# Seven products per 2x2 blocks in twelve of the 22 value-gate pairs of block 2's MLP

## The chip, the core and the metric

The kernel runs on one core of a Trainium2 chip. The metric is the device time of one execution in microseconds. Durations come from one profiled execution, which has a time of its own beside the timed runs.

## What is computed

The reference runs two transformer blocks over 512 tokens of width 1024 in float32. The change concerns the MLP at the end of block 2, a gated MLP of width 2816 with a causal convolution of three taps on the value half:

```
u = rmsnorm_2(x, norm_ffn_w)
up, gate = split(u @ w_ffn_up)          # 1024 -> 2 x 2816
a = causal_dwconv_2(up, ffn_conv_w, ffn_conv_b)
x = x + (silu(a) * gate) @ w_ffn_down   # 2816 -> 1024
return rmsnorm_2(x, norm_final_w)
```

The MLP of block 1 is `x + square(relu(rmsnorm(x) @ w1)) @ w2` with width 4096.

## The kernel before

Everything lies transposed, features on the 128 partitions and the 512 tokens along the row, so x is eight tiles of 128x512. Each float32 product is three matmuls (`mm3`, L461 to L463): both operands are split into a rounded high part (type fp32r) and the low rest, and hi by hi, lo of one by hi of the other and the reverse are summed in PSUM.

**Weights.** `weight_order` lists all 128x128 weight tiles in the order of use; eight tiles are a unit of 512 KB. SP loads units into four `raw` buffers, in program order; ScalarE (ACT) casts each to `whi` (L258), VectorE (DVE) subtracts to get `wlo` (L260). There are five buffers for `whi` and five for `wlo`, and one is free again when TensorE (PE) has done its last matmul with it. `defer(n, f)` puts a step off by n weight tiles.

**Plain pairs.** `hidden2(i)` computes value tile i and gate tile 22+i: two units, `lin` over eight k each, so 2 x 8 x 3 = 48 matmuls of 512 columns into two of the four `mm` banks of PSUM. Then DVE multiplies by the norm's factor `rb` (L1676, into `zp`), ACT and DVE do the three taps (L1585, L1587 twice), ACT the silu (L1678), DVE the product with the gate out of PSUM (L1679), and ACT and DVE split the result (L529, L530). `GROUPS2` cuts the 22 pairs into groups of 8, 8 and 6. After each of the first two groups, with the first pair of the next group ahead of it, eight tiles of the down projection follow (L1691 on DVE, L1692 on POOL); the last group ends in a tail by halves of the tokens.

**Pairs by seven products.** The MLP of block 1 already computes 14 of its 16 pairs of output tiles with `pairg`. It takes a pair's weights and the input as 2x2 blocks (two output tiles by two k tiles; two k tiles by two halves of 256 tokens), and needs seven block products instead of eight: 7 x 4 x 3 = 84 matmuls of 256 columns. The list SEVEN gives the order of the products: 1, 5, 2, 7, 3, 6, 4. The weight side (`seven_steps`, L297 to L318) is two sums and their splits: tiles called `a` (products 1 and 4), `s75s` (5 and 7), `s64s` (6 and 3), each of 1024 columns, and `b` (product 2), of 512. The token side (`rights`, L405 to L416) is made once per MLP, in four steps of two x tiles each. A pair fills four banks of PSUM; ACT copies product 1 out (`c0`, L380), and DVE assembles the results in `q` (L386 to L389).

**What sets the order.** SP keeps the program's order. On the other engines a scheduler places the instructions by its own estimates of when their inputs are there, so a step can stand ahead of work that the code writes first. Each engine then takes its instructions strictly in that order.

Of the kernel before, what the change touches and what calls it, by code (L numbers as in the profile page):

```python
# [9 lines left out]
F32 = mybir.dt.float32  # L10
F32R = mybir.dt.float32r
I32 = mybir.dt.int32
U8 = mybir.dt.uint8
AF = mybir.ActivationFunctionType
ALU = mybir.AluOpType
# [3 lines left out]
T = 512  # L19
# [33 lines left out]
VD = 4  # L53
# [6 lines left out]
def weight_order():  # L60
# [12 lines left out]
    def cols(name, ns, ks):  # L73
        for n in ns:
            for k in ks:
                seq.append((name, k, n))
# [6 lines left out]
    r8 = range(8)  # L83
# [32 lines left out]
    cols("w_mix_out_2", r8, r8)  # L116
    for g, (a, b) in enumerate(GROUPS2):
        for i in range(a + (1 if g else 0), b + (1 if b < 22 else 0)):
            cols("w_ffn_up_2", [i, 22 + i], r8)
        cols("w_ffn_down_2", r8, range(a, b))  # L120
    return seq, seven

# [13 lines left out]
            yield 1, 4 * g + 7, g + 1  # L136


GROUPS2 = [(0, 8), (8, 16), (16, 22)]


# [27 lines left out]
def _build(ctx, tc, nc, A, out, stage):  # L169
# [5 lines left out]
    V, S, G, PE = nc.vector, nc.scalar, nc.gpsimd, nc.tensor  # L175
    cnt = [0]

    def nm(s):
        cnt[0] += 1
        return f"{s}_{cnt[0]}"  # L180

    def t2(dt=F32, shape=(P, T)):
        return ap_.tile(list(shape), dt, tag="t2", bufs=NSLOT, name=nm("t2"))
# [10 lines left out]
    def tinyc(n):  # L194
        return ap_.tile([P, n], F32, tag=nm("tinyc"), bufs=1, name=nm("tinyc"))

    def bank(kind="mm"):
        return pp.tile([P, T], F32, tag=kind, bufs=4, name=nm(kind))
# [21 lines left out]
    def col(name, i=0, n=1):  # L220
        o = COFF[name][0] + i
        return colt[:, o:o + n]
# [210 lines left out]
    def defer(n, fn):  # L433

        late.append((wst["i"] + n, fn))
        late.sort(key=lambda e: e[0])
# [37 lines left out]
    def lin(name, n, ks, mv, ps=None, start=True, stop=True, off=0):  # L474
        if ps is None:
            ps = bank()
        for _ in ling(name, n, ks, mv, ps, start, stop, off):
            pass
        return ps
# [56 lines left out]
    def zpad():  # L536
        zp = ap_.tile([P, T + 4], F32, tag="t2", bufs=NSLOT, name=nm("zp"))
        G.memset(zp[:, 0:4], 0.0)
        return zp
# [92 lines left out]
    def acc_tile():  # L632
        return ap_.tile([P, T], F32, tag="t2", bufs=NSLOT, name=nm("acc"))


    xs = []
# [16 lines left out]
    rb = row_bc(rc, 4)  # L653
# [22 lines left out]
    kf, qf, vf, gv, gu, gate, ys = [], [], [], [], [], [], []  # L676
# [540 lines left out]
    xs = xs2  # L1217
# [86 lines left out]
    xs = xs2  # L1304
# [4 lines left out]
    rops, steps = rights(x, "norm_ffn", xs)  # L1309
# [92 lines left out]
    xs = xs2  # L1402

    rc12, rc, rb, rb1 = tinyc(8), tinyc(4), acc_tile(), acc_tile()
# [178 lines left out]
    def conv3(zp, wname, j):  # L1583
        c = tmp()
        S.activation(c, zp[:, 2:2 + T], AF.Copy, scale=col(wname, 3 * j))  # L1585
        for i in (1, 2):
            V.scalar_tensor_tensor(out=c, in0=zp[:, 2 + i:2 + i + T], scalar=col(wname, 3 * j + i),  # L1587
                                   in1=c, op0=ALU.mult, op1=ALU.add)
        return c
# [76 lines left out]
    xs = xs2  # L1666


    rb = acc_tile()
    wide_later(acc, 1e-5, rb, 3, False)  # L1670

    def hidden2(i):
        ps = lin("w_ffn_up_2", i, range(8), xs)
        psg = lin("w_ffn_up_2", 22 + i, range(8), xs)
        zp = zpad()
        V.tensor_mul(zp[:, 4:], ps, rb)  # L1676
        c = conv3(zp, "ffn_conv_w_2", i)
        S.activation(c, c, AF.Silu, bias=col("ffn_conv_b_2", i))  # L1678
        V.tensor_mul(c, c, psg)  # L1679
        return split(c)  # L1680

    hs = []
    for g, (a, b) in enumerate(GROUPS2):
        hs += [hidden2(i) for i in range(a + (1 if g else 0), b)]
# [10 lines left out]

    a, b = GROUPS2[2]
    nk = b - a
# [25 lines left out]
    for hf in range(2):  # L1723
# [4 lines left out]
        st = {}  # L1728
# [140 lines left out]
```

## Time and profile before

| | us |
|---|---|
| runs, median of 3 (lowest to highest) | 1544.16 (1543.84 to 1545.23) |
| the profiled execution: time | 1543.86 |
| the profiled execution: span, first to last instruction | 1542.1 |
| TensorE busy in the span | 1514.8 |
| VectorE busy | 999.0 |
| ScalarE busy | 674.9 |

The span of the profiled execution is 1.8 us under its own time, and that time is 0.3 us under the median of the runs. Busy times of the engines overlap. A matmul's recorded length contains its drain, so what a matmul costs is read from one start to the next; the same holds in part for DVE and ACT, where the next instruction often starts some 0.1 us before the last one is over.

### The profile page before, as it was taken

The numbers are of one execution on the slowest core, as the hardware profiler recorded it, in microseconds if no ns is written. First come the engines' busy times: TensorE is split into PE (matmuls) and PEld (weight loads), VectorE is DVE, ScalarE is ACT, GpSimd is POOL, SyncE is SP. The second block draws the span as 40 slices with busy tenths as digits, with TensorE's granted clock in tenths as the row PEclk, the third lists the DMA queues.
The fourth block names the chain that finished last, engine by engine and source line by source line (L and its number), as shares of the span: only waits on it lengthen the run. The fifth ranks groups of instructions, "written<-read, shape, count | busy, mean of one in ns | idle before, by whom it ended". The sixth has DMA issues, their size and how long they took to land.

```text
span 1542.1 us, 20324 instructions
## 1 busy us (share of the span) xinstructions
PE 1514.8 (98%) x7904; PEld 1274.9 (83%) x7904; DVE 999.0 (65%) x1623; ACT 674.9 (44%) x1117; POOL 143.5 (9%) x162
## 2 busy tenths in 40 slices
PE   8999999999999999999999999999999999999996
PEld 6888898888888888989888888888888888888886
DVE  6897675554786786767688767335546555555557
ACT  6666555443564353535444444333334331332233
POOL 0002120200201212011400000000020002001101
PEclk9999999999999999999999999999999999999998
DMA  6033335221223323324043222222232222232311
GB/s 254 20 111 100 112 130 197 96 68 55 82 72 106 96 95 109 104 83 137 14 150 131 83 82 83 81 92 92 92 96 96 96 96 96 96 96 92 100 41 56
DMA packets 51505, 149.89 MB, mean 97 GB/s; under 512 B 9552, under 2 KB 14032, under 8 KB 51408
## 3 DMA queue, kind: packets, MB, share of 16 engines
q1 hardware_dynamic: 51264, 148.32, 29.1%
q8 instruction: 62, 1.02, 0.3%
q14 instruction: 35, 0.29, 0.1%
q10 hardware_dynamic: 144, 0.26, 0.1%
HBM read 143.97 MB, written 3.28 MB: 95 GB/s over the span
## 4 chain that ended last, share of the span: by engine, by line
PE 95%; DVE 2%; ACT 2%; issue 1%; DMA 0%; POOL 0%; SPq 0%; DVEq 0%; ACTq 0%; POOLq 0%
PE mm L461 28%; PE mm L462 27%; PE mm L463 27%; PE sm L463 2%; PE sm L461 2%; PE sm L462 2%; ACT whi L258 0%; ACT t L1090 0%; DVE wlo L260 0%; DMA raw<-wts 0%; PE sm L581 0%; PE sm L1576 0%; PE sm L1575 0%; PE sm L1577 0%; PE sm L713 0%
## 5 line engine op out<-in xcount | busy, mean ns | idle before, releaser
L461 PE MATMUL mm<-t,whi 128*128 128x512 f32 (+1 forms) x1888 | 719.9, 381 | 9.1 <-ACT whi L254 7.3
L462 PE MATMUL mm<-t,whi 128*128 128x512 f32 (+1 forms) x1888 | 716.7, 380 | 0.2 <-DVE t L530 0.2
L463 PE MATMUL mm<-t,wlo 128*128 128x512 f32 (+1 forms) x1888 | 716.8, 380 | 0.0
L258 ACT CAST whi<-raw 128x1024 fp32r<-128x1024 f32 x226 | 236.5, 1051 | 432.7 <-PE mm L462 286.2
L461 PEld LDWEIGHTS mm<-t,whi 128*128 128x128 f32 x1888 | 355.3, 188 | 77.9 <-ACT whi L254 7.3
L463 PEld LDWEIGHTS mm<-t,wlo 128*128 128x128 f32 x1888 | 355.3, 188 | 72.1 <-DVE wlo L260 0.8
L462 PEld LDWEIGHTS mm<-t,whi 128*128 128x128 f32 x1888 | 355.2, 188 | 69.6 <-DVE t L530 0.4
L260 DVE TENSOR_TENSOR wlo<-raw,whi 128x1024 fp32r<-128x1024 f32 x219 | 287.4, 1312 | 81.8 <-ACT whi L258 78.8
L575 POOL TENSOR_TENSOR acc<-acc,tmp 128x512 f32<-128x512 f32 (+1 forms) x37 | 52.7, 1432 | 468.2 <-ACT tmp L571 467.9
L1436 DVE TENSOR_TENSOR tmp<-mm,acc 128x512 f32<-128x512 f32 x46 | 31.7, 689 | 48.8 <-PE mm L463 46.8
L1393 POOL TENSOR_TENSOR res<-res,tmp 128x512 f32<-128x512 f32 x24 | 39.0, 1638 | 247.9 <-DVE tmp L1391 217.3
L310 DVE TENSOR_TENSOR wlo<-sraw,whi 128x1024 fp32r<-128x1024 f32 x28 | 38.4, 1375 | 26.5 <-ACT whi L305 26.5
L461 PE MATMUL sm<-t,whi 128*128 128x256 f32 (+1 forms) x176 | 50.4, 286 | 1.8 <-ACT whi L305 1.8
L1676 DVE TENSOR_TENSOR zp<-mm,acc 128x512 f32<-128x512 f32 x22 | 15.2, 691 | 55.0 <-PE mm L463 54.9
L463 PE MATMUL sm<-t,wlo 128*128 128x256 f32 (+1 forms) x176 | 50.4, 286 | 0.0
L462 PE MATMUL sm<-t,whi 128*128 128x256 f32 (+1 forms) x176 | 50.2, 285 | 0.0
L305 ACT CAST whi<-sraw 128x1024 fp32r<-128x1024 f32 x28 | 29.3, 1047 | 45.8 <-PE mm L462 41.0
L1692 POOL TENSOR_TENSOR res<-res,tmp 128x512 f32<-128x512 f32 x16 | 20.7, 1294 | 260.2 <-DVE tmp L1691 260.2
L1679 DVE TENSOR_TENSOR tmp<-tmp,mm 128x512 f32<-128x512 f32 x22 | 15.1, 687 | 43.4 <-PE mm L463 42.6
L1391 DVE TENSOR_TENSOR tmp<-mm,acc 128x512 f32<-128x512 f32 x32 | 21.6, 686 | 26.5 <-PE mm L463 22.6
L1691 DVE TENSOR_TENSOR tmp<-mm,acc 128x512 f32<-128x512 f32 x16 | 11.1, 692 | 39.2 <-PE mm L463 39.2
L461 PEld LDWEIGHTS sm<-t,whi 128*128 128x128 f32 x176 | 33.1, 188 | 2.5 <-ACT whi L305 2.0
(379 smaller groups left out, 1840.2 us busy)
## 6 DMA issues: line engine op xcount, KB each, us to landing
raw<-wts SPq DMA_DIRECT2D x259, 512.0 KB, 3.7
res<-xT SPq DMA_DIRECT2D x16, 256.0 KB, 5.2
yT<-t SPq DMA_DIRECT2D x6, 256.0 KB, 2.3
tmp<-tmp SPq DMA_DIRECT2D x20, 64.0 KB, 2.0
gm<-gm SPq DMA_DIRECT2D x4, 256.0 KB, 5.2
dn<-ch SPq DMA_DIRECT2D x4, 256.0 KB, 2.3
tmp<-memT SPq DMA_DIRECT2D x4, 256.0 KB, 2.6
cst<-const SPq DMA_DIRECT2D x1, 576.0 KB, 6.7
```

The lines of the kernel that those rows point to most:

```text
L258: S.copy(hi, r)
L260: defer(LO, lambda r=r, hi=hi, lo=lo: V.tensor_sub(lo, r, hi.bitcast(F32)))
L305: S.copy(t[n][0], s)
L310: V.tensor_sub(t[n][1], src(), t[n][0].bitcast(F32))
L461: PE.matmul(ps, lhsT=ahi, rhs=bhi, start=start, stop=False)
L462: PE.matmul(ps, lhsT=ahi, rhs=blo, start=False, stop=False)
L463: PE.matmul(ps, lhsT=alo, rhs=bhi, start=False, stop=stop)
L575: eng.tensor_add(acc[:, :w], acc[:, :w], dst[:, :w])
L1391: V.tensor_mul(t, ps, rb2)
L1393: G.tensor_add(x[n], x[n], t)
L1436: V.tensor_mul(t, ps, rb)
L1692: G.tensor_add(x[n], x[n], t)
```

## The change

Twelve pairs of block 2 (`SEVEN2`) go through `pairg`; the ten others stay plain. Their weights are listed in `pair` order, `rights` is called for block 2's x with its steps from 5 weight tiles on, and `hidden7` takes the place of `hidden2`: it draws `q` from `pairg` and does the same convolution, silu, product and split from there, with the sign folded into L1695. All twelve use the banks called `sm`; block 1 alternates between `mm` and `sm`.

```
+SEVEN2 = {3, 4, 6, 7, 9, 10, 12, 13, 15, 16, 18, 19}
...
-            cols("w_ffn_up_2", [i, 22 + i], r8)
+            if i in SEVEN2:
+                pair("w_ffn_up_2", i, 22 + i)
+            else:
+                cols("w_ffn_up_2", [i, 22 + i], r8)
...
+    rops2, steps = rights(x, "norm_ffn_w_2", xs)
+    for j, f in enumerate(steps):
+        defer(5 + VD * (j // 3) + j % 3, f)
+
+    def hidden7(i):
+        hl = (t2(F32R), t2(F32R))
+
+        def then(q):
+            zp = zpad()
+            V.tensor_mul(zp[:, 4:], q[:, :T], rb)
+            st = {}
+
+            def taps():
+                st["c"] = conv3(zp, "ffn_conv_w_2", i)
+
+            def gate():
+                c = st["c"]
+                S.activation(c, c, AF.Silu, bias=col("ffn_conv_b_2", i))
+                defer(1, lambda: V.scalar_tensor_tensor(out=c, in0=q[:, T:], scalar=-1.0, in1=c,
+                                                        op0=ALU.mult, op1=ALU.mult))
+                defer(2, lambda: S.copy(hl[0], c))
+                defer(4, lambda: V.tensor_sub(hl[1], c, hl[0].bitcast(F32)))
+
+            defer(1, taps)
+            defer(2, gate)
+
+        for _ in pairg("w_ffn_up_2", i, 22 + i, rops2, then, "sm"):
+            pass
+        return hl
...
     def hidden2(i):
+        if i in SEVEN2:
+            return hidden7(i)
```

A line of before has a number five higher in the changed kernel, and 37 higher behind `hidden7` (L461 is L466, L258 is L263, L305 is L310, L380 is L385, L1678 is L1715).

On PE, where pair 1 of block 2's MLP ends and pair 2 begins, before reads as follows (`mm_10631` is the gate of pair 1, `mm_10662` the value of pair 2, `t` the split x, `whi` and `wlo` the weights):

```order
L461 MATMUL mm_10631<-t_1981_10454,whi_10590 128x512
L462 MATMUL mm_10631<-t_1982_10455,whi_10590 128x512
L463 MATMUL mm_10631<-t_1981_10454,wlo_10591 128x512
L461 MATMUL mm_10662<-t_1933_10183,whi_10634 128x512
L462 MATMUL mm_10662<-t_1934_10184,whi_10634 128x512
L463 MATMUL mm_10662<-t_1933_10183,wlo_10635 128x512
```

In the changed kernel, at the same place, 12 matmuls of pair 3's product 1 (`sm_10807`) and 9 of its product 5 (`sm_10825`, whose `t` are made by `rights`) stand between the gate of pair 1 and the value of pair 2 (`mm_10707`); these are their last six and what follows:

```order
L466 MATMUL sm_10825<-t_2011_10558,whi_10726 128x256
L467 MATMUL sm_10825<-t_2012_10559,whi_10726 128x256
L468 MATMUL sm_10825<-t_2011_10558,wlo_10727 128x256
L466 MATMUL sm_10825<-t_2019_10589,whi_10726 128x256
L467 MATMUL sm_10825<-t_2020_10590,whi_10726 128x256
L468 MATMUL sm_10825<-t_2019_10589,wlo_10727 128x256
L466 MATMUL mm_10707<-t_1933_10183,whi_10666 128x512
L467 MATMUL mm_10707<-t_1934_10184,whi_10666 128x512
```

So 21 matmuls of the first pair by seven products moved ahead of a whole plain pair.

On ACT, behind the silu of pair 0, before reads so (`whi` from `raw` is the cast of a unit of weights, `t` from `tmp` the high part of a pair's result):

```order
L258 CAST whi_10709<-raw_10632 128x1024
L529 CAST t_2001_10552<-tmp_10546 128x512
L1585 ACTIVATE tmp_10621<-zp_10618,colt 128x512
L258 CAST whi_10740<-raw_10663 128x1024
L1678 ACTIVATE tmp_10621<-tmp_10621,colt 128x512
L529 CAST t_2013_10627<-tmp_10621 128x512
L258 CAST whi_10784<-raw_10707 128x1024
```

In the changed kernel the same stretch holds the casts of the pairs by seven products: `whi_10827` and `whi_10858` are `s75s` and `s64s` of pair 4, `t_2060_10755` is `b` of pair 3, and `tmp_10697` belongs to the plain pair 1:

```order
L310 CAST whi_10827<-sraw_10808 128x1024
L1590 ACTIVATE tmp_10697<-zp_10694,colt 128x512
L310 CAST whi_10858<-sraw_10839 128x1024
L1715 ACTIVATE tmp_10697<-tmp_10697,colt 128x512
L534 CAST t_2045_10703<-tmp_10697 128x512
L310 CAST t_2060_10755<-raw_10708 128x512
L1590 ACTIVATE tmp_10789<-zp_10786,colt 128x512
```

The cast of pair 3's `b` moved behind a cast for pair 4 and behind the whole activation of pair 1. The buffer that `whi_10858` takes is that of pair 3's `s75s`.

## Rows read from the trace of the kernel before

**Rows 1.** The page: PE's busy time, and the chain that ended last, by engine.

```profile
PE 1514.8 (98%) x7904; PEld 1274.9 (83%) x7904; DVE 999.0 (65%) x1623; ACT 674.9 (44%) x1117; POOL 143.5 (9%) x162
...
PE 95%; DVE 2%; ACT 2%; issue 1%; DMA 0%; POOL 0%; SPq 0%; DVEq 0%; ACTq 0%; POOLq 0%
```

**Rows 2.** Stretches of block 2's MLP: length, busy us (instructions) by engine, clock, DMA.

```profile
1159.00:1195.00 36.00, 36.00 (x156) 28.82 (x155) 26.24 (x34) 16.17 (x20) 0.00 (x0) 1.00 0.27 88
1195.00:1260.00 65.00, 65.00 (x283) 52.68 (x282) 33.39 (x42) 22.92 (x29) 0.00 (x0) 1.00 0.30 97
```

**Rows 3.** DVE in time order, plain pairs: start, length, line, idle before [releaser].

```profile
1209.87 0.69 DVE L1676 TENSOR_TENSOR zp<-mm,acc 128x512 f32<-128x512 f32 x1 [2.84 <-PE mm L463]
...
1211.90 1.53 DVE L1587 SCALAR_TENSOR_TENSOR tmp<-zp,colt,tmp 128x512 f32<-128x512 f32 x2
1215.49 0.69 DVE L1679 TENSOR_TENSOR tmp<-tmp,mm 128x512 f32<-128x512 f32 x1 [2.06 <-PE mm L463]
...
1226.61 0.69 DVE L1679 TENSOR_TENSOR tmp<-tmp,mm 128x512 f32<-128x512 f32 x1 [2.06 <-PE mm L463]
```

**Rows 4.** PE in time order: first matmuls of two consecutive block-1 pairs.

```profile
447.39 0.28 PE L461 MATMUL sm<-t,whi 128*128 128x256 f32 x1
...
457.31 0.28 PE L461 MATMUL mm<-t,whi 128*128 128x256 f32 x1
```

**Rows 5.** DVE in time order: preparation and assembly of pairs in block 1.

```profile
556.41 0.68 DVE L387 TENSOR_TENSOR q<-mm,q 128x512 f32<-128x512 f32 x1
557.01 1.21 DVE L310 TENSOR_TENSOR wlo<-raw,whi 128x1024 fp32r<-128x1024 f32 x1
558.14 0.41 DVE L388 TENSOR_TENSOR q<-mm,q 128x256 f32<-128x256 f32 x1
558.48 0.68 DVE L315 TENSOR_TENSOR sraw<-sraw,raw 128x512 f32<-128x512 f32 x1
```

**Rows 6.** PE in time order: where it waited among block 1's pairs.

```profile
441.12 0.39 PE L461 MATMUL mm<-t,t 128*128 128x256 f32 x1 [1.54 <-ACT t L305]
...
469.58 0.39 PE L461 MATMUL sm<-t,whi 128*128 128x256 f32 x1 [1.83 <-ACT whi L305]
...
554.56 0.51 PE L461 MATMUL mm<-t,whi 128*128 128x512 f32 x1 [0.64 <-ACT t L380]
...
639.74 0.50 PE L461 MATMUL mm<-t,whi 128*128 128x512 f32 x1 [0.68 <-ACT t L380]
```

**Rows 7.** ACT in time order, just before two of those waits ended.

```profile
439.50 1.04 ACT L305 CAST whi<-sraw 128x1024 fp32r<-128x1024 f32 x1
440.45 0.61 ACT L305 CAST t<-raw 128x512 fp32r<-128x512 f32 x1
...
553.20 1.04 ACT L258 CAST whi<-raw 128x1024 fp32r<-128x1024 f32 x1
554.15 0.36 ACT L380 COPY t<-mm 128x256 f32<-128x256 f32 x1
```

**Rows 8.** DVE in time order at the start of block 2's MLP.

```profile
1159.10 0.69 DVE L1661 TENSOR_TENSOR res<-res,mm 128x512 f32<-128x512 f32 x1 [2.78 <-PE mm L463]
...
1164.45 0.69 DVE L623 TENSOR_SCALAR tmp<-sm 128x512 f32<-128x512 f32 x1 [0.59 <-PE sm L617]
...
1171.78 0.69 DVE L1676 TENSOR_TENSOR zp<-mm,acc 128x512 f32<-128x512 f32 x1
```

**Rows 9.** DVE in time order: first and last instruction of one step of `rights`, block 1.

```profile
415.90 0.42 DVE L411 TENSOR_TENSOR t<-t,t 128x256 f32<-128x256 f32 x1
...
417.82 0.69 DVE L530 TENSOR_TENSOR t<-t,t 128x512 fp32r<-128x512 f32 x1
```

**Rows 10.** The clock: the last stretch (columns of rows 2), and PE's first matmuls.

```profile
1530.00:1542.00 12.00, 0.70 (x2) 0.30 (x2) 6.84 (x15) 0.45 (x2) 1.74 (x2) 0.63 0.26 87
...
9.63 0.63 PE L463 MATMUL mm<-t,wlo 128*128 128x512 f32 x1
10.06 0.63 PE L461 MATMUL mm<-t,whi 128*128 128x512 f32 x1
```

## The prediction

> **What bounds the kernel now.** I read the page first: PE is busy 98% of the span and holds 95% of the chain that ended last [rows 1], so time is won only by giving PE less to do and lost wherever PE is made to wait. Next, the stretches of block 2's MLP [rows 2]: PE is busy without a gap in both, while DVE is busy 26.2 of 36 us in the first (norm, first three pairs) and 33.4 of 65 us in the second (plain pairs). Then the pace of a plain pair: the gate products L1679 of two pairs start 11.12 us apart, and before each DVE stands idle for 2.06 and 2.84 us, waiting for PE [rows 3]. So DVE and ACT are fed by PE here and cost nothing yet. Last, what a pair by seven products costs where the kernel has them: first matmul to first matmul 9.92 us [rows 4], and the places where PE waited for them [rows 6].
>
> **What is removed.** 48 matmuls of 512 columns become 84 of 256: 11.12 - 9.92 = 1.20 us less PE per pair [rows 3, 4], 12 pairs, **-14.4 us**. All of it lies on the path. It is there in full only if PE never waits, so the rest of the sum is waits.
>
> **What is added to DVE and ACT.** From start to start a DVE instruction on 1024 elements takes 1.13 us, one on 512 0.60, one on 256 some 0.35 [rows 5]. Per pair by seven: preparation 4 x 1.13 + 3 x 0.60 = 6.3, assembly 3 x 0.60 + 0.35 = 2.2, then the product with `rb`, two taps (1.5, [rows 3]), the product with the gate and the low part, 3.3; together 11.8 us against PE's 9.92. A plain pair asks 2 x 1.13 + 3.3 = 5.6 against 11.12. A plain pair and two by seven give DVE 29.2 us in PE's 31.0. In the sum it fits, with little slack; what matters is the order in which things stand, and there I see four places.
>
> **Place 1, ahead of pair 2.** 21 matmuls of pair 3 now stand before pair 2 on PE (first change of order shown above). They need `rights`, and pair 2 itself needs the bank that DVE frees with pair 0's `zp`. Counting from the residual of the last mix tile (1159.1, [rows 8]), DVE must do until that `zp`: seven 1024-wide steps of weights 7.9; residual, split, sums and the like, eight 512-wide, 5.0; the root chain, 1164.45 to 1171.78 less the one 1024-wide step inside it, 6.2 [rows 8]; three steps of `rights` at 1.9 for the first five plus two low parts, 3.1 each [rows 9], 9.3; `zp` 0.6. That is 29.0 us. PE comes there after four units (22.2), two sums over partitions (0.5) and 21 matmuls (2.5), at 25.6 with 0.4 lost since the norm's sum comes later. If DVE never waits, PE waits 3.4 us; if DVE waits for ACT's high parts as it does in block 1's opening, up to 6.1. I take **4.9**, the middle, **plus 0.4**. In the queue behind PE's wait is everything of MLP 2.
>
> **Place 2, inside pair 3.** PE finishes pair 2 (T), ends products 5 and 7 at T+1.8 and wants `b`. ACT (second change of order): cast of `s75s` of pair 4, whose buffer pair 2's gate holds until T, done at T+1.2; first tap of pair 1, T+1.9; cast of `s64s` of pair 4, free only after product 7, T+2.9; silu of pair 1, which waits for two taps on DVE that stand behind the low part of `s75s` (1.1 + 1.5), T+4.7; product and low part in between, high part of pair 1, T+6.3; `b`, T+6.9. PE waits 5.1, and 0.4 more for `b`'s low part on DVE. The same order in block 1 (cast of `sraw`, then `b` at once, [rows 7]) cost 1.54 [rows 6]; here an activation chain of a plain pair stands between. If DVE's part were free, ACT alone would leave 2.9. I take **5.5** (2.9 to 5.6), since each link is an instruction in a fixed order.
>
> **Place 3, pairs 15 and 16.** Here too `b` of pair 15 stands behind the cast of `s64s` of pair 16, which waits for pair 15's product 7, and behind one 512-wide cast: 1.0 + 0.5 + 0.6 after product 7, 2.3, plus 0.6 for the low part; and 0.5 at pair 16's start. **3.4** (2.3 to 3.6).
>
> **Place 4, starts of second pairs.** Pairs 4, 7 and 13 follow a pair that used the same four banks. Product 1 needs `c0` copied, product 2 the third assembly step, and on ACT `c0` stands behind a cast that waits for the end of the pair before. The like cost 0.64 and 0.68 in block 1, where the copy stood behind a cast on ACT [rows 6, 7]. By the same walk: pair 4 0.9, pairs 6 and 7 1.2, pairs 12 and 13 0.6; **2.7** (0 to 4). Pairs 9, 10, 18 and 19 have their weights split under the down tiles and cost nothing; if that cover went they would cost what 6 and 7 do, 1.2 each time.
>
> **The clock.** The idle of 1.83 us in block 1 [rows 6] left PE's pace as it was: 11.12 / 48 = 0.23 us from one matmul of 512 columns to the next [rows 3]. At the end of the run PE is all but idle and the mean granted clock is 0.63 [rows 10], so it fell to its lower level; at the start, at that level, such matmuls stand 0.43 apart [rows 10]; the run's first eight do, which is 8 x 0.20 = 1.6 us, and I take that for the price of a fall. Places 1 and 2 have idles of 4 to 5 us, longer than any in the trace before its end. Two falls are 3.2; some 0.8 of it comes back as DVE catches up before pair 4. I take **2.4** (0 to 4.5). The Trainium skill (TensorE: Matmul & The Clock Gate, Part 1: The HAM clock gate) says that half rate is the default state, that activity lifts it and that an idle stretch brings it back, which speaks against a change that trades matmuls for waits. By the trace's longest harmless idle alone the sum would be 2.4 us less, by the page's rule as it stands. The last stretch agrees with the page; whether the idles of places 1 and 2 are of that kind, no run here shows.
>
> **The sum.** DMA: bytes and units are the same, SP's order too; nothing. POOL: only the same clears. So 0.4 + 4.9 + 5.5 + 3.4 + 2.7 + 2.4 = 19.3 of waits against 14.4 gained: +4.9. On the profiled execution's own 1543.9 that gives **1548.8 us**; this execution is 0.3 us under the median, which changes nothing. Low ends together: 8.6 of waits, 1538.1; high ends: 0.4 + 6.1 + 5.6 + 3.6 + 4 + 4.5 = 24.2, 1553.7.
>
> **Rivals.**
> *The waits are there but short*: DVE keeps pace as in the sum of works and the clock holds; 9 to 15 us of waits, 1538 to 1545. For it: DVE's overlap from start to start is often better than I count. Against: place 2 is an order, not a load.
> *Faster, as in block 1*: its 14 pairs cost PE five waits, 1.54 + 1.83 + 0.64 + 0.68 [rows 6] and one of 0.18, 4.9 us in all, 0.35 a pair. Twelve at that rate are 4.2, so 1543.9 - 14.4 + 4.2 = 1533.7. It decides if pair 1's silu and high part are done before product 7, so that `b` follows the `s64s` cast at once and place 2 shrinks to 1.5. Against: the silu's taps wait for a buffer that pair 2 holds.
> *Slower still, DVE is the bound*: by recorded lengths a triple asks DVE 13.0 + 13.0 + 6.0 = 32.0 us against 31.0, and casts beside POOL's work take longer; five triples lose 5 us beyond the high sum's middle, 1554 to 1560.
> *It doesn't do what it says*: the order has 432 more rows on PE, 12 x 36, so it does.
>
> **How the numbers follow.** A difference of 0.2%, 3.1 us, is what a measurement of this kernel can tell from none: faster is under 1541.1, slower over 1547.2. The forecast (1546 to 1553) 0.47, of which 0.06 lies under 1547.2; short waits 0.27, of which 0.07 under 1541.1; block 1's rate 0.12; DVE bound 0.14. Faster 0.12 + 0.07 = 0.19; same 0.20 + 0.06 = 0.26; slower 0.41 + 0.14 = 0.55. The range 1539 to 1555 leaves out block 1's rate and about half of the DVE case, 0.2. Cases of both signs: the forecast's own range is 1546 to 1553.
>
> **What would show it.** In the changed profile: `sm` groups of L466 to L468 with 1008 more matmuls of 256 columns, 576 fewer of 512; PE idle before pair 2 ended by DVE (`t` or `zp`), 4 to 6 us; idle inside pair 3 ended by ACT's 512-wide cast L310, about 5 us; some 2 to 3 us at pair 15 by the same line; a granted clock under 1.00 in the stretch of the first pairs. Wrong would be PE idle under 10 us in MLP 2, or waits that L263 or DMA end.

## The result: 0.5% slower

| | before | changed |
|---|---|---|
| median of 5 runs, us | 1544.16 (1543.44 to 1545.23) | 1551.35 (1550.25 to 1555.27) |
| changed to before | | 1.0053, 95% interval 1.0037 to 1.0070 |
| profiled execution, us | 1543.86 | 1555.27 |
| its span | 1542.1 | 1553.5 |

The forecast was 1548.8 us with a range of 1539 to 1555, and slower as the likeliest sign. The median lies 7.2 us over before, the profiled execution 11.4; it is the slowest of its five, and where its surplus comes from stands at the end of the next section.

### The profile page after: what moved, and what is told of

Same layout as the page of the kernel before. It is cut to its first block, busy times and chain, and to the rows that moved or that the text cites. A ratio compares the mean times of both kernels' runs of the same rounds, so it can differ in the third digit from the quotient of the medians.

```text
span 1553.5 us, 21399 instructions
## 1 busy us (share of the span) xinstructions
PE 1512.2 (97%) x8336; PEld 1292.5 (83%) x8336; DVE 1080.4 (70%) x1759; ACT 705.8 (45%) x1169; POOL 147.9 (10%) x162
## 4 chain that ended last, share of the span: by engine, by line
PE 88%; DVE 6%; ACT 3%; issue 1%; DMA 1%; SPq 0%; POOL 0%; DVEq 0%; ACTq 0%; POOLq 0%
PE mm L466 23%; PE mm L468 23%; PE mm L467 23%; PE sm L468 4%; PE sm L466 4%; PE sm L467 4%; DMA raw<-wts 1%; ACT whi L263 1%; DVE wlo L315 1%; DVE wlo L265 1%; ACT whi L310 1%; ACT t L1095 0%; DVE wlo L267 0%; PE sm L586 0%; DVE t L1807 0%
## 5 line engine op out<-in xcount | busy, mean ns | idle before, releaser
L466 PE MATMUL mm<-t,whi 128*128 128x512 f32 (+1 forms) x1696 | 646.6, 381 | 10.3 <-ACT whi L259 6.7
L468 PE MATMUL mm<-t,wlo 128*128 128x512 f32 (+1 forms) x1696 | 643.2, 380 | 1.9 <-DVE wlo L267 1.4
L467 PE MATMUL mm<-t,whi 128*128 128x512 f32 (+1 forms) x1696 | 642.9, 379 | 0.2 <-DVE t L535 0.2
L466 PEld LDWEIGHTS mm<-t,whi 128*128 128x128 f32 x1696 | 320.2, 189 | 71.2 <-ACT whi L259 6.7
L468 PEld LDWEIGHTS mm<-t,wlo 128*128 128x128 f32 x1696 | 320.2, 189 | 67.3 <-DVE wlo L267 2.7
L467 PEld LDWEIGHTS mm<-t,whi 128*128 128x128 f32 x1696 | 320.3, 189 | 61.5 <-DVE t L538 0.5
L263 ACT CAST whi<-raw 128x1024 fp32r<-128x1024 f32 x202 | 211.3, 1051 | 303.3 <-PE mm L467 138.6
L265 DVE TENSOR_TENSOR wlo<-raw,whi 128x1024 fp32r<-128x1024 f32 x189 | 236.5, 1252 | 78.1 <-ACT whi L263 77.7
L466 PE MATMUL sm<-t,whi 128*128 128x256 f32 (+1 forms) x464 | 132.0, 285 | 4.2 <-ACT t L534 2.3
L467 PE MATMUL sm<-t,whi 128*128 128x256 f32 (+1 forms) x464 | 131.7, 284 | 0.5 <-DVE t L535 0.5
L468 PE MATMUL sm<-t,wlo 128*128 128x256 f32 (+1 forms) x464 | 131.7, 284 | 0.0
L310 ACT CAST whi<-sraw 128x1024 fp32r<-128x1024 f32 x52 | 54.5, 1048 | 88.0 <-PE mm L467 69.3
L466 PEld LDWEIGHTS sm<-t,whi 128*128 128x128 f32 x464 | 88.1, 190 | 5.9 <-ACT t L534 2.5
L467 PEld LDWEIGHTS sm<-t,whi 128*128 128x128 f32 x464 | 88.2, 190 | 1.6 <-DVE t L535 0.7
L468 PEld LDWEIGHTS sm<-t,wlo 128*128 128x128 f32 x464 | 88.2, 190 | 0.4
L310 ACT CAST whi<-raw 128x1024 fp32r<-128x1024 f32 x26 | 27.3, 1050 | 67.7 <-PE mm L467 37.0
L466 PE MATMUL sm<-t,t 128*128 128x256 f32 (+1 forms) x156 | 47.0, 302 | 7.3 <-ACT t L310 7.0
L302 DVE TENSOR_TENSOR sraw<-raw,raw 128x1024 f32<-128x1024 f32 x26 | 33.0, 1269 | 25.3 <-DMA raw<-wts 25.2
```

The costliest lines, as they stand in the source:

```text
L263: S.copy(hi, r)
L265: defer(LO, lambda r=r, hi=hi, lo=lo: V.tensor_sub(lo, r, hi.bitcast(F32)))
L302: V.tensor_tensor(t["s75"].rearrange("p (a b) -> p a b", a=2), r3, r1[:, T:].unsqueeze(1).to_broadcast([P, 2, T]), op=ALU.add)
L310: S.copy(t[n][0], s)
L466: PE.matmul(ps, lhsT=ahi, rhs=bhi, start=start, stop=False)
L467: PE.matmul(ps, lhsT=ahi, rhs=blo, start=False, stop=False)
```

## The profile after

First the page: busy time by engine, and the chain that ended last. They answer to [rows 1].

```profile
PE 1512.2 (97%) x8336; PEld 1292.5 (83%) x8336; DVE 1080.4 (70%) x1759; ACT 705.8 (45%) x1169; POOL 147.9 (10%) x162
...
PE 88%; DVE 6%; ACT 3%; issue 1%; DMA 1%; SPq 0%; POOL 0%; DVEq 0%; ACTq 0%; POOLq 0%
```

PE is 2.6 us less busy, not 14.4, and 7 points of the chain have gone from PE to the others: there are waits now, and something has stretched the matmuls. The stretches of [rows 2] show both (length, busy us and instructions of PE, its weight loads, DVE, ACT, POOL, then the granted clock, DMA):

```profile
1159.00:1195.00 36.00, 31.35 (x138) 25.30 (x137) 29.30 (x48) 17.11 (x23) 1.42 (x6) 0.95 0.17 59
1195.00:1260.00 65.00, 59.73 (x372) 54.23 (x371) 51.53 (x71) 30.05 (x41) 0.41 (x4) 0.92 0.27 90
1191.20:1198.00 6.80, 6.10 (x14) 4.79 (x15) 3.52 (x6) 3.35 (x4) 0.10 (x1) 0.50 0.00 0
```

In before PE was busy for all of both stretches at a clock of 1.00. Now it is idle for 4.65 and 5.27 us of them, the granted clock is 0.95 and 0.92, and for the 6.8 us of the third line it is 0.50, the lower of its two levels (1.2 in place of 2.4 GHz). PE in order of time, the places at which it waited and what followed the second (start, length, idle before and its releaser):

```profile
1188.70 0.39 PE L466 MATMUL sm<-t,whi 128*128 128x256 f32 x1 [2.34 <-ACT t L534]
...
1189.59 0.39 PE L467 MATMUL sm<-t,whi 128*128 128x256 f32 x1 [0.50 <-DVE t L535]
...
1191.90 0.80 PE L466 MATMUL mm<-t,whi 128*128 128x512 f32 x1 [1.81 <-DVE zp L1713]
1192.49 0.63 PE L467 MATMUL mm<-t,whi 128*128 128x512 f32 x1
1192.92 0.63 PE L468 MATMUL mm<-t,wlo 128*128 128x512 f32 x1
...
1212.64 0.58 PE L466 MATMUL sm<-t,t 128*128 128x256 f32 x1 [4.81 <-ACT t L310]
...
1388.44 0.39 PE L466 MATMUL sm<-t,t 128*128 128x256 f32 x1 [2.16 <-ACT t L310]
...
1389.86 0.58 PE L468 MATMUL sm<-t,t 128*128 128x256 f32 x1 [0.33 <-DVE t L315]
```

The first three are place 1, ended by the parts of `rights` (L534, L535) and by pair 0's `zp`; 1212.64 is place 2 and 1388.44 place 3, both ended by the cast of `b` (L310). Behind 1191.90 the matmuls of 512 columns stand 0.43 us apart where they stood 0.23. ACT in order of time ahead of 1212.64 (columns as above) is the queue that the forecast walked through:

```profile
1205.92 1.05 ACT L310 CAST whi<-sraw 128x1024 fp32r<-128x1024 f32 x1 [0.59 <-PE mm L467]
1206.88 0.72 ACT L1590 ACTIVATE tmp<-zp,colt 128x512 f32<-128x512 f32 x1
1207.80 1.04 ACT L310 CAST whi<-sraw 128x1024 fp32r<-128x1024 f32 x1 [0.21 <-PE sm L467]
1209.71 0.72 ACT L1715 ACTIVATE tmp<-tmp,colt 128x512 f32<-128x512 f32 x1 [0.86 <-DVE tmp L1592]
1211.45 0.62 ACT L534 CAST t<-tmp 128x512 fp32r<-128x512 f32 x1 [1.01 <-DVE tmp L1716]
1211.97 0.61 ACT L310 CAST t<-raw 128x512 fp32r<-128x512 f32 x1
```

`b`, the last line, needs nothing but its raw weights, and stands behind two casts for pair 4 and the activation of pair 1 (tap, silu, high part); both casts, the silu and the high part each wait for another engine.

**The account.** All matmuls are in both traces (7904 and 8336), so the MLP, with some 85 us ahead of it, can be measured on PE from the 5801st matmul, the same product in every kernel, to the last: 1074.01 to 1530.43 in before, 1076.52 to 1541.84 after, 456.4 and 465.3 us, +8.9. The gain is there: away from waits and falls a matmul of 512 columns takes 0.232 us and one of 256 takes 0.118 in both traces (medians from start to start), so twelve pairs save 12 x (48 x 0.232 - 84 x 0.118) = 14.7 us, for 14.4 in the forecast. What PE spent beyond that pace therefore grew by 14.7 + 8.9 = 23.6 us. Of these, waits of 0.25 us or more ahead of the final norm make 13.6. The clock stands at half in three stretches, 1191.2 to 1198.0, 1211.7 to 1218.5 and 1389.1 to 1392.5; PE worked in 6.1, 5.8 and 3.1 us of them, and half of that was lost, 7.5. The last 2.5 are shorter waits and restarts, found as a remainder and not measured. The other 2.5 us of the profiled execution's 11.4 lie ahead of the MLP: 1.0 us in the first 200 us, and 1.5 where the clock fell in block 1 (471.0 to 474.4), behind a wait that before has too [rows 6, the wait of 1.83], without a fall.

## Experiments

My theory: PE's gain is whole, and is lost in waits that the fixed orders of DVE and ACT make at places 1 to 3, and again in the clock that falls behind them. Rivals: the clock is worth little (A), DVE is the bound (B), a pair gains less than its matmuls say (C). In this table the MLP is the stretch of the account above, from the profile of each run.

| run | median, us | to before, 95% interval | MLP, us |
|---|---|---|---|
| before | 1544.16 | | 456.4 |
| changed | 1551.35 | 1.0037 to 1.0070 | 465.3 |
| `rights` early | 1537.42 | 0.9943 to 0.9968 | 449.2 |
| `b` first | 1547.44 | 1.0011 to 1.0029 | 459.7 |
| without 3 and 4 | 1544.21 | 0.9990 to 1.0009 | 455.1 |
| four pairs | 1545.30 | 0.9995 to 1.0012 | 457.3 |
| pauses on purpose | 1603.98 | 1.0364 to 1.0392 | 515.5 |
| `rights` early, `b` first | 1534.08 | 0.9915 to 0.9943 | 446.2 |
| `rights` early, four pairs | 1541.46 | 0.9968 to 0.9987 | 452.8 |
| without 4 | 1545.91 | 0.9999 to 1.0016 | 458.2 |
| both kinds of banks | 1545.42 | 0.9995 to 1.0013 | 456.4 |
| fourteen pairs | 1541.94 | 0.9974 to 0.9991 | 454.5 |
| filler products | 1553.12 | 1.0040 to 1.0067 | 465.8 |
| never two in a row | 1535.63 | 0.9930 to 0.9955 | 448.3 |

### Places 1 and 2 taken away: `rights` early

```
     for n in range(8):
         ...
+        if n % 2 and n < 7:
+            for j, f in enumerate(steps[3 * (n // 2):3 * (n // 2) + 3]):
+                defer(2 + 2 * j, f)
 ...
-    for j, f in enumerate(steps):
-        defer(5 + VD * (j // 3) + j % 3, f)
+    for j, f in enumerate(steps[9:]):
+        defer(5 + j, f)
```

> Three of the four steps of `rights` are made while the mix tiles run, as soon as their two x tiles are there, and only the last one in the MLP. DVE's work in total is the same. In the order of the engines all of pair 3 then stands behind pair 2 on PE, and `b` of pair 3 stands ahead of both casts of pair 4 on ACT; nothing changes at pair 15. Theory (waits from the fixed order at places 1 and 2, and a clock that falls after them): the waits of 4.65 us ahead of pair 2 and 4.81 us inside pair 3 go, and with them the two falls of 6.83 us each at half pace, 6.8 us; from 1551.4 that is 1535.1, with place 3 (2.5 us and its fall of 3.41 us) unchanged. Rival A (the waits go, but the clock falls were worth only the 2.4 us of the forecast): 1539.5. Rival B (DVE is the bound of the pairs, and what it doesn't lose at places 1 and 2 it loses later): at most the 6 us of `rights` that leave the MLP, 1545 or more.

1537.42 us, 0.44% faster than before. The same two stretches (columns as above), and the waits that are left at place 3:

```profile
1159.00:1195.00 36.00, 36.00 (x164) 29.37 (x163) 30.61 (x45) 17.37 (x23) 0.30 (x3) 1.00 0.18 61
1195.00:1260.00 65.00, 64.47 (x434) 58.81 (x433) 54.36 (x70) 30.07 (x41) 0.30 (x3) 1.00 0.33 114
```

```profile
1371.39 0.39 PE L466 MATMUL sm<-t,t 128*128 128x256 f32 x1 [2.13 <-ACT t L310]
...
1372.81 0.39 PE L468 MATMUL sm<-t,t 128*128 128x256 f32 x1 [0.44 <-DVE t L315]
```

Both waits and both falls are gone. The MLP is 16.2 us shorter than in the changed kernel, where the theory said 16.3. In the medians it is 13.9: the profiled execution of the changed kernel is 3.9 us over its median, that of this one 0.4 under. Rival B falls: DVE does the same work (1083.7 us busy against 1080.4), is denser in the second stretch (54.4 us of 65), and PE runs through. Place 3 is there as before with 2.13 us, but this time no fall follows it; so 1.5 of the 16.2 us are place 3's fall in the changed kernel, and places 1 and 2 account for some 14.6. Moving `rights` moves two things at once, the load on DVE and, through the scheduler's estimates, `b` on ACT; the run doesn't tell them apart.

### Place 3 taken away: `b` first

```
+        if order[8 * u][0] == "w_ffn_up_2":
+            return op, [
+                both(s75, hi("b", b), hi("a", a)),
+                both(lo("b", b), lo("a", a), hi("s75s", c)),
+                both(s6, s4),
+                both(lo("s75s", c), hi("s64s", d)),
+                lo("s64s", d),
+                end,
+            ]
```

> In block 2 alone the split of `b` is written ahead of the other steps of a pair's preparation. On ACT `b` of pair 15 then stands ahead of the casts of pair 16; at pair 3 it still stands behind the cast of `s64s` of pair 4 and the activation of pair 1, as in the changed kernel. Theory: place 3 goes, 2.16 + 0.33 us of wait and half of the 3.41 us at half pace, 4.2 us together: 1547.2; places 1 and 2 as they were. Rival A (the clock is worth little): 1548.9. Rival B (DVE is the bound): 1551, since DVE has the same work.

1547.44 us, as the theory said (1547.2). Place 3's two waits are gone; a wait of 1.25 us at product 2 of pair 13, ended by DVE's assembly, stands where 0.28 stood. At place 2, where the order of ACT didn't change, the wait is again 4.81 us, ended by the same line.

### The first two pairs left plain, and four pairs alone

```
-SEVEN2 = {3, 4, 6, 7, 9, 10, 12, 13, 15, 16, 18, 19}
+SEVEN2 = {6, 7, 9, 10, 12, 13, 15, 16, 18, 19}     # without 3 and 4
+SEVEN2 = {9, 10, 18, 19}                           # four pairs
```

> SEVEN2 without 3 and 4: ten pairs by seven products, the first of them pair 6. `rights` is long done by then, and `b` of pair 6 stands ahead of the casts of pair 7 on ACT. Two pairs less give back 2 x 1.20 = 2.4 us. Theory: 1551.4 + 2.4 - 4.65 - 4.81 - 6.8 = 1537.5, place 3 unchanged. Rival A (the clock is worth 2.4): 1541.9. Rival B (DVE is the bound, about 1 us for each triple of pairs): 1549 to 1552.

> SEVEN2 = {9, 10, 18, 19} alone: the pairs whose weights are split under the down tiles or beside plain pairs. It measures the gain of a pair by itself. Theory: 4 x 1.20 = 4.8 us less than the kernel before and no wait over 0.5 us in the MLP: 1539.4. Rival C (a pair by seven gains less than its matmuls say, by waits at its start of 0.5 each and by slower matmuls): 1541.5. If `rights` alone costs something at the norm, in place of place 1: 1541 or more, and PE idle before pair 2 or 3.

Both missed: 1544.21 where 1537.5 was expected, 1545.30 where 1539.4 was. Both have one wait more than I had thought of. PE of the kernel with four pairs, its only wait of more than 0.3 us in the MLP before the final norm, and DVE of the same kernel ahead of it:

```profile
1187.25 0.50 PE L466 MATMUL mm<-t,whi 128*128 128x512 f32 x1 [3.41 <-DVE zp L1713]
```

```profile
1184.77 1.22 DVE L265 TENSOR_TENSOR wlo<-raw,whi 128x1024 fp32r<-128x1024 f32 x1 [0.82 <-ACT whi L263]
1185.91 0.68 DVE L535 TENSOR_TENSOR t<-t,t 128x512 fp32r<-128x512 f32 x1
1186.51 0.68 DVE L1713 TENSOR_TENSOR zp<-mm,acc 128x512 f32<-128x512 f32 x1
```

No pair by seven stands near: `rights` itself, three steps of it ahead of pair 0's `zp`, holds DVE until 1186.51 where before had its `zp` at 1171.78 [rows 8], and two plain pairs then fill all four `mm` banks before one comes free. A fall of 3.4 us follows. Without 3 and 4 the same wait (3.41 us) and the same fall stand there, and place 3's wait (2.17 us, this time without a fall). So a large part of place 1 is not the order of PE, as I had put it in these two expectations, but the second condition of the forecast, pair 0's bank, and it is there with four pairs as with twelve. The gain of a pair is untouched. The first matmul of pair 9 and the first one behind pair 10, in the kernel with four pairs:

```profile
1311.41 0.28 PE L466 MATMUL sm<-t,whi 128*128 128x256 f32 x1
...
1331.25 0.40 PE L466 MATMUL mm<-t,whi 128*128 128x512 f32 x1
```

That is 19.84 us for two, 9.92 a pair as in the forecast; pairs 18 and 19 take 19.78. So four pairs gain 4.8 us, the wait of 3.41 and half of the fall's 3.4 cost 5.1, and some 0.6 of short waits remain: +0.9, the difference of the MLP. Rival C falls, and the third possibility in the second expectation, that `rights` costs something at the norm, holds.

### The same four pairs with `rights` early

The edit is that of the first run, with SEVEN2 = {9, 10, 18, 19}.

> SEVEN2 = {9, 10, 18, 19} with three steps of `rights` beside the mix tiles. With the four pairs alone PE waited 3.4 us ahead of pair 2, for `zp` of pair 0 from DVE, though no product by seven stands there, and the clock then fell for 3.4 us. Theory: `rights` on DVE makes that wait; without it 1545.3 - 3.4 - 1.7 = 1540.2 or, by the sum, 1544.2 - 4.8 = 1539.4. Rival (the wait comes from the weights' preparation or the order of PE): 1545 as before, with the same wait ahead of pair 2.

1541.46 us, and no wait over 0.3 us in the MLP before the final norm. `zp` of pair 0 on DVE (columns as above) now stands 9.6 us earlier, counted in both traces from the first matmul of the stretch:

```profile
1175.98 0.69 DVE L1716 TENSOR_TENSOR zp<-mm,acc 128x512 f32<-128x512 f32 x1
```

The MLP is 4.5 us shorter than with `rights` late, for 5.1 expected, and 3.6 shorter than before's for a gain of 4.8. The other 1.2 are not at the pairs by seven, which take 19.88 us for two: the plain matmuls are slightly slower here (see *Open* in the next part).

### What a pause costs: eight on purpose

```
+IDLE = {2: [], 4: [128], 6: [512], 11: [512] * 2, 13: [512] * 4, 15: [], 18: [512, 128], 20: [512] * 6}
 ...
+        V.tensor_scalar_mul(c[:, :w], last["g"][:, :w], 0.0)
+        for j, w in enumerate(IDLE[i]):
+            d = t2(F32R if j == len(IDLE[i]) - 1 else F32)
+            S.copy(d[:, :w], c[:, :w])
+            c = d
 ...
+            PE.matmul(ps, lhsT=c[:, :P], rhs=xs[0][0], start=True, stop=False)
```

> The kernel before with eight pauses made on purpose: ahead of pairs 2, 4, 6, 11, 13, 15, 18 and 20 of block 2's MLP, PE has to wait for a chain of copies that starts from the gate bank of the pair before (one small copy on DVE, then none to six on ACT) and ends in a product with zeros that opens each of the pair's two banks; the results don't change. Sixteen matmuls are added, 3.7 us. By the lengths of DVE's and ACT's copies (0.69 behind the product with the gate, then 0.3 to 0.7, then 0.6 each) the pauses should be about 1.3, 1.7, 2.3, 2.9, 4.1, 1.3, 2.6 and 5.3 us, 21.5 together, each at PE's full pace before and after. It measures what a pause costs through the clock. Theory: the clock falls after the long ones and not after the short ones, for 3.4 or 6.8 us at half pace each time, which costs half of that; with 3 to 5 falls 1544.2 + 3.7 + 21.5 + 6 to 15 = 1575 to 1584. Rival A (the clock is worth little): 1569 to 1571, and no stretch at half pace beyond one.

The pauses came out longer than planned, 37.1 us in place of 21.5. PE at the eight places (columns as above):

```profile
1186.81 1.22 PE L1686 MATMUL mm<-t,t 128*128 128x512 f32 x2 [4.38 <-DVE t L1678]
...
1214.43 1.22 PE L1686 MATMUL mm<-t,t 128*128 128x512 f32 x2 [3.33 <-ACT t L1681]
...
1244.21 1.15 PE L1686 MATMUL mm<-t,t 128*128 128x512 f32 x2 [4.05 <-ACT t L1681]
...
1351.39 1.22 PE L1686 MATMUL mm<-t,t 128*128 128x512 f32 x2 [4.71 <-ACT t L1681]
...
1382.85 1.22 PE L1686 MATMUL mm<-t,t 128*128 128x512 f32 x2 [5.96 <-ACT t L1681]
...
1410.97 0.73 PE L1686 MATMUL mm<-t,t 128*128 128x512 f32 x2 [2.96 <-DVE t L1678]
...
1495.65 1.22 PE L1686 MATMUL mm<-t,t 128*128 128x512 f32 x2 [4.39 <-ACT t L1681]
...
1528.01 1.22 PE L1686 MATMUL mm<-t,t 128*128 128x512 f32 x2 [7.26 <-ACT t L1681]
```

And the stretch before the first of them, and those behind the first and the sixth (columns of the stretches above):

```profile
1150.00:1182.00 32.00, 32.00 (x138) 25.60 (x137) 22.18 (x30) 12.80 (x17) 4.02 (x11) 1.00 0.30 99
1186.90:1189.50 2.60, 2.60 (x6) 2.06 (x7) 0.00 (x0) 0.00 (x0) 0.00 (x0) 0.50 0.15 60
...
1411.60:1414.80 3.20, 3.20 (x9) 2.53 (x8) 0.00 (x0) 0.00 (x0) 0.00 (x0) 0.50 0.32 127
```

Behind each of the eight, the shortest with 2.96 us too, the clock stood at 0.50 for a while. The MLP grew by 59.0 us; 3.7 are the sixteen added matmuls and 37.1 the pauses, which leaves 18.2, or 2.3 us for a pause. Of these, 16.9 are the clock: PE worked 33.8 us in the eight falls, at half pace. Rival A falls: such a pause costs its own length and 2.3 us more, where the forecast had 1.6 for a fall and gave half of one back. The Trainium skill (TensorE: Matmul & The Clock Gate, HAM oscillation — how this bites in real kernels) tells of a kernel that pays for a throttled start after each wait between groups of matmuls; all eight pauses agree with that.

### Both edits: `rights` early and `b` first

> Both edits in one: three steps of `rights` beside the mix tiles, and `b` ahead in a pair's preparation. Theory: places 1, 2 and 3 are gone and the clock stays up in the MLP; what is left is 12 x 1.20 of gain, some 2 us at the starts of pairs and about 1 us of DVE work at the norm: 1544.2 - 14.4 + 3 = 1533, or by the run with `rights` early alone 1537.4 less place 3 (2.6) = 1534.8. Rival B (DVE is the bound and a wait comes back elsewhere): 1537 or more, with a new wait on DVE's lines of over 1 us in the MLP.

1534.08 us, between the two values of the theory (1533 and 1534.8): 0.71% faster than before and the best of the kernels run. What is left of waits over 0.4 us on PE in the MLP ahead of the final norm (four; two are shown), and the second stretch:

```profile
1237.31 0.50 PE L477 MATMUL mm<-t,wlo 128*128 128x512 f32 x1 [0.42 <-DVE wlo L267]
...
1316.79 0.39 PE L475 MATMUL sm<-t,t 128*128 128x256 f32 x1 [1.23 <-DVE q L402]
```

```profile
1195.00:1260.00 65.00, 64.58 (x443) 59.41 (x442) 55.02 (x72) 31.34 (x42) 0.30 (x3) 1.00 0.36 114
```

DVE is busy 55.0 of 65 us here, 85%, and still isn't the bound. The MLP is 10.2 us shorter than before's: of the 14.4 gained 4.2 are lost, 2.5 of them in waits of 0.4 us and more.

### Place 2 without place 1: pair 4 left plain

SEVEN2 as in the changed kernel, without 4.

> SEVEN2 without 4: eleven pairs. Pair 3 still has 21 matmuls ahead of pair 2, so place 1 stays. Inside pair 3 there is no `s64s` of pair 4 on ACT any more, and in the order of PE 22 matmuls of the now plain pair 4 stand ahead of product 2 of pair 3, so `b` has 5 us more. Theory (place 1 and place 2 are two waits, each with its own fall of the clock): place 2 goes, 4.81 us and some 2.9 us of its fall, and 1.2 us of gain: 1551.4 + 1.2 - 4.8 - 2.9 = 1544.9, with place 1 still 4.6 us and its stretch at half pace. Rival (place 2 is the echo of place 1, so that DVE's lag shows elsewhere): 1549 or more.

1545.91 us where the theory said 1544.9, but not by the way it said. PE in order of time, the last wait of place 1 and a new one at pair 6:

```profile
1188.11 0.50 PE L466 MATMUL mm<-t,whi 128*128 128x512 f32 x1 [0.87 <-DVE zp L1713]
...
1235.75 0.38 PE L466 MATMUL sm<-t,t 128*128 128x256 f32 x1 [2.17 <-ACT t L310]
```

Place 2 is gone, as said. But place 1 shrank too, from 4.65 to 2.04 us (1.17 and 0.87) and without a fall, since DVE no longer makes pair 4's sums ahead of `zp` (L302, L320 and L323, 2.3 us of its time); and at pair 6 `b` now stands behind the casts of pair 7, which cost 2.17 and 0.46 us and a fall. Two waits at pair 13, for DVE's assembly (0.82 and 1.09 us), are new too, and place 3's wait of 2.16 us had no fall here. That the total came out near is chance. What holds is the kind of wait. In the traces of all kernels here `b` stands nine times behind the cast of the next pair's `s64s`, and each time PE waits for it, 2.13 to 4.81 us; where it stands ahead of that cast, PE never waits for it for 0.25 us or more, but for the kernel with filler products below. Which pair it hits changes with the edit.

### Place 4: both kinds of banks

```
-        for _ in pairg("w_ffn_up_2", i, 22 + i, rops2, then, "sm"):
+        for _ in pairg("w_ffn_up_2", i, 22 + i, rops2, then, "mm" if i in ALT2 else "sm"):
+ALT2 = {4, 7, 10, 13, 16, 19}
```

> As the run with `rights` early and `b` first, and the second pair of each two (4, 7, 10, 13, 16, 19) uses the banks `mm` in place of `sm`. What was left of waits there was 1.23 us at pair 13, for DVE's assembly of pair 12 in the same banks, and three times 0.43. Theory (place 4 is the banks): these 2.5 us go, 1534.1 - 2.5 = 1531.6. Rival (with `mm` shared, the plain pairs wait for the assembly in their place): 1534 or more, with new waits on `mm` of plain pairs.

1545.42 us, 11.3 slower than without this edit: the rival was right, and by more than it said. ACT just before the longest new wait, and PE at its end:

```profile
1247.14 0.62 ACT L1710 CAST t<-tmp 128x512 fp32r<-128x512 f32 x1 [0.30 <-DVE tmp L1708]
1247.66 0.37 ACT L395 COPY t<-mm 128x256 f32<-128x256 f32 x1
```

```profile
1248.08 0.75 PE L476 MATMUL mm<-t,whi 128*128 128x512 f32 x1 [2.42 <-ACT t L395]
```

The plain pair behind waits for a bank of the pair by seven, which ACT's copy of `c0` (L395) frees, and that stands in the queue behind the high part of an earlier result. This happens three times at length (2.42, 1.85, 2.42), with two falls, and twice more for 0.89 and 0.43 us. Keeping `sm` for the pairs by seven was the better choice.

### More pairs, and fewer

`rights` early and `b` first in both; SEVEN2 = {3, 4, 6, 7, 8, 9, 10, 12, 13, 15, 16, 18, 19, 21} and {3, 5, 7, 9, 10, 12, 14, 16, 18, 20}.

> `rights` early and `b` first, with pairs 8 and 21 by seven products too, 14 in all. By the gain of a pair, 1.20 us: 1534.1 - 2.4 = 1531.7. Rival B (DVE has no more to give where three such pairs stand in a row, 6 to 8 and 18, 19, 21): 1533.5 or more, with new waits on DVE's lines at pairs 8 or 21 or in the last half of the down projection.

> `rights` early and `b` first, with SEVEN2 = {3, 5, 7, 9, 10, 12, 14, 16, 18, 20}: ten pairs, and but for 9 and 10, whose weights are split under the down tiles, a plain pair behind each. A pair by seven and a plain one ask DVE for 5.6 + 11.8 = 17.4 us and PE for 21.0. Theory (places 2 to 4 are the wait of a pair for the one before it): no wait over 0.5 us is left, 1544.3 + 0.5 - 10 x 1.20 = 1532.8, a little under the twelve pairs with the same edits (1534.1) though two pairs less gain. Rival (a pair's start costs some 0.4 wherever it stands): 1536 to 1537.

Fourteen pairs gave 1541.94, 7.9 us slower than twelve. ACT ahead of the tail of the MLP, and PE's first matmul there:

```profile
1491.26 0.62 ACT L1709 CAST t<-tmp 128x512 fp32r<-128x512 f32 x1 [0.76 <-DVE tmp L1707]
```

```profile
1491.93 0.58 PE L475 MATMUL mm<-t,whi 128*128 128x256 f32 x1 [4.16 <-ACT t L1709]
```

Pair 21 is the last; behind it stands only the tail, which needs its result at once, and assembly, taps, silu, product and high part come after its last matmul with nothing to hide them: 4.16 us and a long fall. At pair 6 there is a wait of 1.89 us, with a fall, that twelve pairs didn't have. The rival had the direction, but both waits end on ACT's lines and none on DVE's.

Ten pairs with a plain one behind each gave 1535.63; its only waits over 0.3 us before the final norm are at the one place where two stand together, pair 10 behind pair 9:

```profile
1313.37 0.39 PE L475 MATMUL sm<-t,whi 128*128 128x256 f32 x1 [1.39 <-DVE q L400]
...
1316.57 0.38 PE L475 MATMUL sm<-t,t 128*128 128x256 f32 x1 [1.27 <-DVE q L402]
```

So the theory holds for the eight single pairs, and what it missed are 2.7 us at the two that stand together: 1532.8 + 2.7 = 1535.5. There PE waits for DVE's assembly (`q`, L400 and L402), which empties the banks of the pair before. The single pairs show the gain by itself, from the first matmul of pair 3 to that of pair 4 (plain) and of pair 5:

```profile
1192.62 0.28 PE L475 MATMUL sm<-t,whi 128*128 128x256 f32 x1
...
1202.55 0.40 PE L475 MATMUL mm<-t,whi 128*128 128x512 f32 x1
...
1213.71 0.28 PE L475 MATMUL sm<-t,whi 128*128 128x256 f32 x1
```

That is 9.93 us by seven products and 11.16 plain. All eight single pairs take 9.91 to 9.95.

### Work in place of idle time

```
+                if name == "w_ffn_up_2" and n1 in FILL:
+                    fb = bank()
+                    for f in range(FILL[n1]):
+                        PE.matmul(fb[:, :H], lhsT=lops[7][0][:, :P], rhs=ops[3]["V7"][0],
+                                  start=f == 0, stop=f == FILL[n1] - 1)
+FILL = {3: 36}
```

> The changed kernel with 36 products of 256 columns added inside pair 3, into a free bank that nobody reads: 36 x 0.118 = 4.25 us of PE, in the order of PE ahead of product 2, where it waited 4.81 us with nothing to do and then ran for some 2.9 us' worth at half pace. The order of ACT changes by one row: `b` of pair 3 then stands ahead of the cast of `s64s` of pair 4. Theory (the clock falls because PE is idle, and that is a cost beside the wait): the wait shrinks to under 1 us, the filler takes its place, and the fall that followed it goes: 1551.4 - 4.8 + 4.25 + 0 to 0.8 - 2.9 = 1548 to 1549. Rival A (the fall costs nothing, or comes from something other than idle time): 1551 to 1552. If the fall only moves, 1551 and a stretch at half pace of the same length near 1212.

1553.12 us, where 1548 to 1549 was expected. At the place itself the theory holds. PE at product 2 of pair 3, and further on at pair 6:

```profile
1208.35 0.39 PE L472 MATMUL sm<-t,t 128*128 128x256 f32 x1 [0.27 <-ACT t L311]
...
1242.53 0.39 PE L472 MATMUL sm<-t,t 128*128 128x256 f32 x1 [2.16 <-ACT t L311]
```

```profile
1208.00:1215.00 7.00, 6.56 (x51) 6.01 (x50) 5.92 (x8) 4.65 (x7) 0.00 (x0) 1.00 0.24 76
```

The wait fell from 4.81 to 0.27 us, and the clock stays at 1.00 behind it. The 36 products took 4.3 us; without them PE would have stood idle for these, since `b` came no earlier (ACT has its cast at 1207.68). But the added rows shifted the scheduler's order once more: `b` of pair 6 now stands behind casts of pair 7, as in the kernel without pair 4, and that wait (2.16 and 0.45 us) and a fall take back what was gained. The run shows that place 2's fall belonged to its idle time, since with PE at work there it didn't come; as a remedy the filler is useless.

## Why the prediction was right, and which term was off

| term | forecast, us | profiled execution, us |
|---|---|---|
| gain of 12 pairs | -14.4 | -14.7 |
| norm's sum | 0.4 | under 0.25 |
| place 1, ahead of pair 2 | 4.9 | 2.34 + 0.50 + 1.81 = 4.65 |
| place 2, inside pair 3 | 5.5 | 4.81 |
| place 3, pairs 15 and 16 | 3.4 | 2.16 + 0.33 = 2.49 |
| place 4, starts of pairs | 2.7 | 3 x 0.46 + 0.28 = 1.66 |
| the clock | 2.4 | 7.5 |
| short waits and restarts (remainder) | not counted | 2.5 |
| sum, in the MLP | +4.9 | +8.9 |

**Right.** The gain per pair: 9.88 to 9.96 us for a single pair by seven with `b` first, where the forecast had 9.92. The three places and the sizes of their waits: they come from instructions in a fixed order, and could be walked through link by link from durations in the trace of before. The releasers are right at places 2 and 3; of place 1 the first 2.34 us were ended by ACT's high parts of `rights` (L534), where DVE was named. The removal runs fit the sizes: places 1 and 2 account for some 14.6 us, where their waits (9.46) and half of PE's 11.9 us at half pace make 15.4; and in the run without place 3 the MLP lost 5.6 us, of which place 3 makes 4.0 (2.49 and half of 3.1) and less work at half pace behind places 1 and 2 (9.2 us in place of 11.9) makes 1.4. DVE as the bound fell, as the sum of its works had it.

**The mis-sized term: the clock.** Two steps failed. The price of a fall was taken as 1.6 us from the run's first eight matmuls, and 0.8 of two falls' 3.2 was given back for what DVE catches up; PE worked 6.1 and 5.8 us at half pace behind places 1 and 2, which is 3.0 and 2.9 us, and eight pauses cost 2.3 on average. And place 3 was counted as harmless, since the longest idle among the pairs in the trace of before, 1.83 us, had left the pace as it was (so it had, by the granted clock; the pace that was cited is that of pairs 740 us later); 2.16 us were followed by a fall worth 1.5 us in this execution, and the very wait of 1.83 us in block 1 by one of 1.5. The range for this term was 0 to 4.5 and should have reached over 7. The waits were 3.3 us too high together, the gain 0.3 too low, and 2.5 were not counted. So that the median fell into the range is in part luck, by errors of both signs; the profiled execution, with the fall in block 1, lies just over it.

**Slips that changed little.** The low ends add up to 9.0, not 8.6, since the norm's 0.4 is left out (1538.5); eight 512-wide instructions at 0.60 are 4.8, not 5.0; at place 3, 1.0 + 0.5 + 0.6 is 2.1, not 2.3, against 2.16 measured. And it is DVE's low parts, not ACT's casts, that take longer beside POOL (figures at the end).

**Place 1's cause.** The forecast named two conditions, the 21 matmuls of pair 3 ahead of pair 2, which need `rights`, and pair 0's bank, and its sum ran on the second, on DVE's work up to `zp`. That is borne out: with no pair by seven near, `rights` alone made PE wait 3.41 us for `zp`. What was wrong is my first theory after the result: it took the 21 matmuls for the cause, and so the expectations for the runs without pairs 3 and 4 and with four pairs missed. In the changed kernel PE waits for both in turn, 2.84 us for the parts of `rights` and 1.81 for `zp`; the remedy was to make `rights` earlier.

**Wrong: place 4's mechanism.** Pairs 4, 7 and 13 don't wait for `c0` at their start. The waits of 0.46 us stand at the first plain pair behind two by seven, which PE begins between the two, for the low part of its first weights (L267); in other orders it is the assembly that PE waits for (1.23 to 1.39 us, L400 and L402). Giving the second pair other banks, which my mechanism would have made harmless, cost 11 us.

**Open.** What is left over beyond waits and falls was not followed up. A part of it isn't waits at all: in the kernels with `rights` early a plain pair that waits for nothing takes 11.16 to 11.18 us (11.28 with both kinds of banks), where before takes 11.12 and the kernels with `rights` late 11.10 to 11.11. With four pairs this is most of the 1.2 us that were missing. Why these matmuls are slower no run shows. Whether place 2 without any help from `rights` would go if `b` alone stood first on ACT there wasn't tried: the scheduler didn't move it.

## What to carry to other kernels

A change that takes work from the bounding engine and gives it to its feeders gains what its matmuls say only where every product on that engine finds its operand ready; walk through the feeders' queues in order, since an operand that needs nothing can stand behind several that wait. Make what is needed once, like `rights`, in the stage before, where the feeders have room: that edit turned 0.5% slower into 0.4% faster, and with `b` first 0.7%. And price a wait on TensorE in such a stretch at its length and, from 3 us on, 1.5 to 3 us of half clock more; near 2 us it may be either.

## What the runs showed of the hardware

Which waits of TensorE the fall of the clock followed, counted over the profiles of all fourteen kernels here: behind the 28 waits of 1.48 to 1.54 us ahead of block 2 and the seven of 1.09 to 1.39 in the MLP, never; behind the wait of 1.83 us in block 1, in 5 of 14 profiles, before's among those without; behind the waits of 1.85 to 2.42 us in the MLP, those at place 3, at pair 6 and for the banks, in 7 of 11; behind the thirteen of 2.96 to 7.26 us, each time. Place 1, where several waits follow each other, is not in this count; it had a fall wherever its waits added up to 4 us or more. So one and the same wait, that of block 1, costs 1.8 us in one execution and 3.4 in another, and the times of one kernel spread with the granted clock: the kernel without pair 4 ran in 1543.4 us at a mean granted clock of 0.998 and in 1547.3 at 0.994. The lower clock often sets in while PE is still idle (1.0 us before the end of place 2's wait), and that part of it costs nothing.

Beside POOL's work some of DVE's instructions take longer. In the trace of before 224 low parts of 1024 columns (L260, L310) that POOL's instructions don't touch took 1.22 us (median, 1.23 at most), and the 32 with POOL at work for over half of their time 2.26 (median); ACT's casts of the same width took 1.05 us either way.
